# Moving the low-part weight tiles of a two-part float32 matmul kernel from 64 to 76 bytes off the other operands

## The chip, the core and the metric

The kernel runs on one NeuronCore of a Trainium2 chip. The metric is the device time of one execution in microseconds, as the median of several runs: 2093.12 us before the change (three runs, 2093.07 to 2093.68). The profiled execution, from which all durations below are taken, is one more run of the same program.

## What is computed

The reference is a two-layer decoder trunk on 256 tokens of width 2048, all in float32. Cut to its matrix products:

```python
D_MODEL = 2048; SEQ = 256; G_W = 1536; D_FF = 5632; MEM_W = 512; Q_RANK = KV_RANK = 512

def conv_ffn(h, w_up, cw, cb, w_down):          # in both layers
    a = h @ w_up                                 # 2048 -> 11264
    ...
    return (jax.nn.silu(gate) * val) @ w_down    # 5632 -> 2048

# layer 0
z = h @ w_in_a[l]                                # 2048 -> 3584: gate, value, memory queries
main = spatial_gating(z[..., :G_W], z[..., G_W:2 * G_W], g_v[l], w_sp[l], b_sp[l])
# layer 1
z = h @ w_in_b[j]                                # 2048 -> 1024
main = mla_attention(...)                        # low-rank attention with w_uq, w_uk, w_uv
# both layers
mo = memory_attention(q_m, mem, g_mem[l], w_mem_kv[l])
x = x + jnp.concatenate([main, mo], axis=-1) @ w_out[l]
x = x + conv_ffn(rmsnorm(x, g_ffn[l]), w_ffn_up[l], conv_w[l], conv_b[l], w_ffn_down[l])
```

Most of the arithmetic is the two feed-forward blocks (w_ffn_up and w_ffn_down), then w_in_a and w_out.

## The kernel before

**Two parts for each operand.** TensorE multiplies in the type fp32r, which keeps fewer bits than float32. So each operand is split into a high part (the value as fp32r holds it) and a low part (the rest), and a product is the sum of three matmuls: high by high, high by low, low by high. An activation operand is one tile of 128 partitions by 512: the high part of the 256 tokens in the first 256 columns, the low part in the last 256. These tiles are named xhl (the residual stream), h (the hidden layer of the feed-forward block), mainhl, memhl, qhl and chl. A weight chunk of 128 by 1024 arrives in a tile raw by a DMA of 512 KB from SP's queue (`chunk`, L107); ScalarE (ACT) copies it to its high part, tile whi (L117, or L122 with a gain), and VectorE (DVE) subtracts to get the low part, tile wlo (L118, or L123 with a gain). Four buffers of raw, whi and wlo turn over.

**Two ways to run a product.** In `gemm_fm` the weights are the operand that TensorE loads (128 columns), and the activations stream past it. `mm_fm` issues two kinds of matmul: L158 loads a block of whi and streams all 512 columns of the activation tile (high and low together), L162 loads a block of wlo and streams the 256 high columns alone. It issues all L162 of a group of chunks in a row, and all L158 in a row, in alternating order from group to group; away from the ends of a product two groups meet, so that 32 matmuls of one kind follow 32 of the other. In `gemm_tm` it is the other way round: the activations are loaded (128 tokens), and the weights stream, 512 columns wide: L213 (high by whi), L214 (high by wlo), L215 (low by whi). In the last product of the program a few of these are 256 columns wide. A wlo tile is loaded by `gemm_fm`, by the queries' product and by the stacked key weights (L872), and streamed by `gemm_tm`.

**Where the tiles lie.** In this text the place of an operand is its byte address within a partition, modulo 256. The tiles whi, raw, wlo and all six activation tiles begin at place 96. The columns taken from them begin at multiples of 512 bytes, so every operand of L158, L213, L214 and L215 is at place 96. The wlo tile is 1088 columns of 4 bytes long (4352 bytes, 17 times 256), although 1024 are used. `low_tile` returns the first 1024 columns where the tile will stream (`moves=True`), and 1024 columns from the 16th on where it will be loaded. So the wlo weights of L162 and L872 are at place 96 + 64 = 160, and those that stream at 96.

**What sets the order.** A scheduler orders each engine's instructions; only the first product and the last one have an order written out by hand. Semaphores tie a matmul to the DVE and ACT instructions that write its weights, and these to the matmuls that last used the buffer.

Of the kernel before, what the change touches and what calls it, by code (L numbers as in the profile page):

```python
# [69 lines left out]
class Kernel:  # L70
# [21 lines left out]

    def low_tile(self, moves=False):
        w = self.wp.tile([P, 1088], F32R, tag="wlo", name=self.uid("wlo"), bufs=4)
        return w[:, :1024] if moves else w[:, 16 : 16 + 1024]


    def chunk(self, src, nk, ncol, gains=None, heads=None, raw=None, moves=False):
# [1025 lines left out]
```

## Time and profile before

| | before |
|---|---|
| median of three runs | 2093.12 us |
| the profiled execution | 2094.34 us |
| its span, first to last instruction | 2092.6 us |
| TensorE matmul busy (PE) | 2082.2 us |
| weight loads busy (PEld) | 1821.7 us |
| VectorE busy (DVE) | 1458.7 us |
| ScalarE busy (ACT) | 1139.0 us |
| GpSimd busy (POOL) | 398.9 us |
| bytes moved by DMA | 392.01 MB, mean 187 GB/s |
| granted TensorE clock, mean | 0.999 |

The profiled execution is 1.7 us longer than its span, and 1.2 us longer than the median. In the rows of the profile, PE is a matmul and PEld the weight load that goes with it; "ps<-xhl,wlo" is a matmul that reads tiles xhl and wlo and adds to a PSUM tile ps. Loads overlap the matmul before. A matmul's own duration (281 ns, say) is its time from start to modelled end, and matmuls are pipelined, so that the next one starts long before: what counts for the time is the distance from one start to the next, which this text calls the pace. It is read from the timeline view, which merges equal instructions that follow each other: the start of one row less the start of the row before, divided by that row's count.

### The profile page before, as it was taken

How to read it: one execution, taken by the hardware profiler on the slowest of the kernel's cores; microseconds unless marked ns; L12 is line 12 of the kernel's file. 1: busy time of each engine (PE TensorE's matmuls, PEld its weight loads, DVE VectorE, ACT ScalarE, POOL GpSimd, SP SyncE). 2: the span in 40 equal slices, each digit the busy share in tenths (PEclk: the TensorE clock that was granted, in tenths of full speed). 3: DMA queues.
4: the chain of work that ended last, by engine and by line, in shares of the span. 5: the costliest groups of instructions: out<-in, count | busy, mean ns of one | idle time of the engine just before them, and what ended most of it. 6: DMA issues, size and time to landing. Idle time of an engine off the chain costs nothing.

```text
span 2092.6 us, 31012 instructions
## 1 busy us (share of the span) xinstructions
PE 2082.2 (100%) x11614; PEld 1821.7 (87%) x11614; DVE 1458.7 (70%) x2150; ACT 1139.0 (54%) x1747; POOL 398.9 (19%) x387
## 2 busy tenths in 40 slices
PE   9999999999999999999999999999999999999998
PEld 8888888888888888888888888888888888888886
DVE  6755767777756777567798875777765677746775
ACT  6754654555535655445655664456553565535554
POOL 0100133312101211012244121421210122201220
PEclk9999999999999999999999999999999999999999
DMA  8665555656556565556555534555655556555554
GB/s 272 197 216 159 161 195 188 191 188 195 191 192 191 181 201 188 194 185 190 190 192 182 176 106 159 185 190 181 192 194 194 186 188 194 196 196 189 184 191 152
DMA packets 208092, 392.01 MB, mean 187 GB/s; under 512 B 14334, under 2 KB 23876, under 8 KB 207812
## 3 DMA queue, kind: packets, MB, share of 16 engines
q1 hardware_dynamic: 207364, 388.98, 57.3%
q8 instruction: 91, 1.49, 0.3%
q10 hardware_dynamic: 576, 1.05, 0.2%
q14 instruction: 61, 0.50, 0.1%
HBM read 387.88 MB, written 2.10 MB: 186 GB/s over the span
## 4 chain that ended last, share of the span: by engine, by line
PE 99%; DMA 0%; ACT 0%; DVE 0%; issue 0%; ACTq 0%
PE ps L158 51%; PE ps L162 26%; PE ps L215 6%; PE ps L213 6%; PE ps L214 6%; PE ps L949 0%; PE ps L947 0%; PE ps L575 0%; PE ps L610 0%; DMA raw<-in_w_mem_kv 0%; PE ps L432 0%; PE ps L979 0%; PE ps L760 0%; PE ps L872 0%; PE ps L970 0%; PE ps L1051 0%
## 5 line engine op out<-in xcount | busy, mean ns | idle before, releaser
L118 DVE TENSOR_TENSOR wlo<-raw,whi 128x1024 fp32r<-128x1024 f32 x660 | 842.5, 1286 | 468.1 <-ACT whi L117 346.0
L117 ACT ACTIVATE whi<-raw 128x1024 fp32r<-128x1024 f32 x660 | 695.6, 1058 | 692.3 <-PE ps L158 511.3
L158 PE MATMUL ps<-xhl,whi 128*128 128x512 f32 x3264 | 765.0, 390 | 0.0
L158 PEld LDWEIGHTS ps<-xhl,whi 128*128 128x128 f32 x3264 | 605.1, 188 | 121.2
L662 POOL TENSOR_TENSOR a<-js,rbc 128x256 f32<-128x256 f32 x176 | 232.1, 1331 | 1094.1 <-DVE js L264 998.5
L162 PEld LDWEIGHTS ps<-xhl,wlo 128*128 128x128 f32 x3264 | 400.8, 189 | 8.4
L162 PE MATMUL ps<-xhl,wlo 128*128 128x256 f32 x3264 | 404.8, 281 | 0.0
L158 PE MATMUL ps<-h,whi 128*128 128x512 f32 x704 | 164.7, 390 | 0.0
L665 ACT ACTIVATE c<-a,cT 128x256 f32<-128x256 f32 x176 | 105.2, 598 | 98.6 <-POOL a L662 97.0
L158 PEld LDWEIGHTS ps<-h,whi 128*128 128x128 f32 x704 | 130.5, 188 | 26.0
L214 PE MATMUL ps<-wlo,h 128*128 128x512 f32 x354 | 137.1, 388 | 0.0
L213 PE MATMUL ps<-whi,h 128*128 128x512 f32 x354 | 137.0, 388 | 0.0
L215 PE MATMUL ps<-whi,h 128*128 128x512 f32 x354 | 136.6, 388 | 0.0
L158 PE MATMUL ps<-mainhl,whi 128*128 128x512 f32 x512 | 120.1, 390 | 0.0
L158 PEld LDWEIGHTS ps<-mainhl,whi 128*128 128x128 f32 x512 | 94.8, 188 | 18.9
L667 DVE SCALAR_TENSOR_TENSOR c<-a,cT,c 128x254 f32<-128x254 f32 x176 | 101.0, 586 | 0.0
L666 DVE SCALAR_TENSOR_TENSOR c<-a,cT,c 128x255 f32<-128x255 f32 x176 | 91.7, 540 | 12.9 <-ACT c L665 12.7
L123 DVE SCALAR_TENSOR_TENSOR wlo<-raw,gT,whi 128x512 fp32r<-128x512 f32 x112 | 87.1, 819 | 19.3 <-ACT whi L122 17.5
L122 ACT ACTIVATE whi<-raw,gT 128x512 fp32r<-128x512 f32 x112 | 74.7, 723 | 31.6 <-PE ps L158 14.2
L264 DVE TENSOR_TENSOR js<-ps,cr 128x256 f32<-128x256 f32 x209 | 82.2, 415 | 12.4 <-POOL a L662 12.4
L262 ACT ACTIVATE cr<-ps 128x256 f32<-128x256 f32 x243 | 79.7, 374 | 15.7 <-PE ps L158 12.1
L162 PEld LDWEIGHTS ps<-h,wlo 128*128 128x128 f32 x704 | 86.5, 189 | 1.9
(259 smaller groups left out, 1859.6 us busy)
## 6 DMA issues: line engine op xcount, KB each, us to landing
raw<-in_w_ffn_up SPq DMA_DIRECT2D x352, 512.0 KB, 3.5
raw<-in_w_ffn_down SPq DMA_DIRECT2D x176, 512.0 KB, 4.3
raw<-in_w_out SPq DMA_DIRECT2D x64, 512.0 KB, 3.5
raw<-in_w_in_a SPq DMA_DIRECT2D x56, 512.0 KB, 4.0
raw<-in_w_mem_kv SPq DMA_DIRECT2D x31, 512.0 KB, 3.8
raw<-in_w_in_b SPq DMA_DIRECT2D x16, 512.0 KB, 3.5
raw<-in_w_kv_a SPq DMA_DIRECT2D x9, 512.0 KB, 4.2
raw<-in_w_uq SPq DMA_DIRECT2D x12, 384.0 KB, 3.3
```

The costliest lines, as they stand in the source:

```text
L117: nc.scalar.activation(hi[:, :n], raw[:, :n], AF.Copy)
L118: nc.vector.tensor_tensor(lo[:, :n], raw[:, :n], hi[:, :n].bitcast(F32), ALU.subtract)
L123: nc.vector.scalar_tensor_tensor(lo[:, s], raw[:, s], gains[k], hi[:, s].bitcast(F32), ALU.mult, ALU.subtract)
L158: mm(acc[:, :], wh, x, start=first, stop=last)
L162: mm(acc[:, S:], wl, x[:, :S], start=False, stop=False)
L213: mm(acc, xh, wh, start=first, stop=False)
L214: mm(acc, xh, wl, start=False, stop=False)
L215: mm(acc, xl, wh, start=False, stop=last)
L662: nc.gpsimd.tensor_tensor(a, self.join(acc), rb, ALU.mult)
L665: nc.scalar.activation(c, a, AF.Identity, scale=w(2), bias=w(3))
L666: nc.vector.scalar_tensor_tensor(c[:, 1:], a[:, : S - 1], w(1), c[:, 1:], ALU.mult, ALU.add)
L667: nc.vector.scalar_tensor_tensor(c[:, 2:], a[:, : S - 2], w(0), c[:, 2:], ALU.mult, ALU.add)
```

## The change

One number changes: the low part of weights that are loaded begins at column 19 of its tile instead of column 16, so 76 bytes from the tile's start instead of 64, at place 172 instead of 160.

```diff
     def low_tile(self, moves=False):
         w = self.wp.tile([P, 1088], F32R, tag="wlo", name=self.uid("wlo"), bufs=4)
-        return w[:, :1024] if moves else w[:, 16 : 16 + 1024]
+        return w[:, :1024] if moves else w[:, 19 : 19 + 1024]
```

The tile keeps its size, and all tiles keep their addresses. No instruction is added, removed or moved: on all five engines the instructions stand in the same order before and after. What differs is the address of the loaded operand of 4728 matmuls L162 and 8 of the 16 matmuls L872, and the address to which VectorE writes these low parts (L118, L123, and those of the queries and the stacked weights). Streaming low parts (L214) stay at place 96.

## The prediction

> **What bounds the kernel now.** I read the page's busy times first, then the clock, the chain that ended last, and what TensorE waited for.
>
> ```profile
> PE 2082.2 (100%) x11614; PEld 1821.7 (87%) x11614; DVE 1458.7 (70%) x2150; ACT 1139.0 (54%) x1747; POOL 398.9 (19%) x387
> ...
> PEclk9999999999999999999999999999999999999999
> ...
> PE ps L158 51%; PE ps L162 26%; PE ps L215 6%; PE ps L213 6%; PE ps L214 6%; PE ps L949 0%; PE ps L947 0%; PE ps L575 0%; PE ps L610 0%; DMA raw<-in_w_mem_kv 0%; PE ps L432 0%; PE ps L979 0%; PE ps L760 0%; PE ps L872 0%; PE ps L970 0%; PE ps L1051 0%
> ```
>
> ```profile
> PE ps L513 <- DVE ones L312: 1.1, 1, 1.1
> PE ps L356 <- DMA graw<-in_g_mem: 0.3, 1, 0.3
> PE ps L979 <- ACT pT L972: 0.3, 1, 0.3
> PE ps L158 <- DVE memhl L482: 0.2, 1, 0.2
> ```
>
> TensorE is busy over the whole span at a granted clock that never falls, and the waits of its matmuls (second view: total, times, longest) come to 2 us in all. So the time is the sum of TensorE's paces, and nothing else. 26% of the chain is L162, the only large group whose operand the change moves; a nanosecond on its pace counts in full. The groups of L162:
>
> ```profile
> L162 PE MATMUL ps<-xhl,wlo 128*128 128x256 f32 x3264 | 404.8, 281 | 0.0
> ...
> L162 PE MATMUL ps<-h,wlo 128*128 128x256 f32 x704 | 87.0, 281 | 0.0
> L162 PE MATMUL ps<-mainhl,wlo 128*128 128x256 f32 x512 | 63.4, 281 | 0.0
> ...
> L162 PE MATMUL ps<-memhl,wlo 128*128 128x256 f32 x128 | 17.6, 283 | 0.1
> ...
> L162 PE MATMUL ps<-qhl,wlo 128*128 128x256 f32 x72 | 9.7, 280 | 0.0
> ...
> L162 PE MATMUL ps<-chl,wlo 128*128 128x256 f32 x48 | 7.0, 282 | 0.0
> ```
>
> That is 3264 + 704 + 512 + 128 + 72 + 48 = 4728 matmuls. The eight of L872 are too few to matter.
>
> **The pace of L162, in three conditions.** Timeline rows (start, length, engine, line) from the middle of the program, with the low weights 64 bytes off what streams:
>
> ```profile
> 1402.77 3.93 PE L162 MATMUL ps<-xhl,wlo 128*128 128x256 f32 x32
> 1406.54 7.44 PE L158 MATMUL ps<-xhl,whi 128*128 128x512 f32 x32
> 1413.82 3.93 PE L162 MATMUL ps<-xhl,wlo 128*128 128x256 f32 x32
> ```
>
> (1406.54 - 1402.77) / 32 = 117.8 ns for L162, and 7.28 / 32 = 227.5 ns for the 512 wide L158. By this pace the 4728 take 557 us, which agrees with 26% of the span. Second, the end of the last product, where loaded and streaming operands are at one place (0 bytes off) and the matmuls are as wide as L162's:
>
> ```profile
> 2080.76 0.39 PE L214 MATMUL ps<-wlo,h 128*128 128x512 f32 x1
> ...
> 2082.57 0.28 PE L213 MATMUL ps<-whi,h 128*128 128x256 f32 x1
> ...
> 2083.29 0.28 PE L213 MATMUL ps<-whi,h 128*128 128x256 f32 x1
> ```
>
> Six intervals in 0.72 us: 120.0 ns at 0 bytes off. (The eight 512 wide ones before took 1.81 / 8 = 226.3 ns.) Third, a short run of L162 in the attention part, again 64 bytes off:
>
> ```profile
> 1195.40 1.08 PE L162 MATMUL ps<-chl,wlo 128*128 128x256 f32 x8
> 1196.31 0.63 PE L158 MATMUL ps<-chl,whi 128*128 128x512 f32 x2
> ```
>
> 0.91 / 8 = 113.8 ns. So the same instruction on operands at the same places runs at two paces, and equal places are slower than either. The durations (shortest, median, longest) of the same three stretches, in the same order, from the views of the lines in those windows:
>
> ```profile
> L162 PEld LDWEIGHTS ps<-xhl,wlo x32: 187/188/192, 1402.5 to 1406.3; 128*128 128x128 f32 x32
> L162 PE MATMUL ps<-xhl,wlo x32: 280/281/282, 1402.8 to 1406.4; 128*128 128x256 f32 x32
> ```
>
> ```profile
> L214 PEld LDWEIGHTS ps<-wlo,h x4: 188/192/192, 2082.6 to 2083.6; 128*128 128x128 f32 x4
> L214 PE MATMUL ps<-wlo,h x4: 283/283/283, 2082.7 to 2083.8; 128*128 128x256 f32 x4
> ```
>
> ```profile
> L162 PEld LDWEIGHTS ps<-chl,wlo x8: 187/188/188, 1195.2 to 1196.1; 128*128 128x128 f32 x8
> L162 PE MATMUL ps<-chl,wlo x8: 276/276/281, 1195.4 to 1196.2; 128*128 128x256 f32 x8
> ```
>
> The pace goes with two marks: a load that sometimes takes 192 ns instead of 188, and a matmul that takes 276, 281 or 283. At 0 bytes off nearly all loads are long, at 64 bytes some, in the short stretch none.
>
> Last, how fast a load can be repeated when little streams: L760 streams only 128 columns.
>
> ```profile
> 196.83 2.28 PE L760 MATMUL ps<-wT,vn 128*128 128x128 f32 x19
> ...
> L760 PE MATMUL ps<-wT,vn x48: 270/275/275, 189.8 to 208.3; 128*128 128x128 f32 x48
> ```
>
> (2280 - 275) / 18 = 111.4 ns. At 117.8 ns L162 runs 6.4 ns above that.
>
> **How the place can act: a supposition.** A load reads 512 bytes of a partition in about 111 ns, and the matmul that streams meanwhile reads 1024 bytes in about 118, twice as fast. If reads at equal places hinder each other, the stream gains 512 bytes on the load, two rounds of 256, and passes it two or three times: at 0 bytes off the third meeting falls into nearly every load, at 64 bytes it falls at the edge, in some loads and not in others. Twelve bytes more are 12 / 512 x 111.4 = 2.6 ns later. The rows above fit this, but none shows a meeting.
>
> [...]
>
> **The change part by part.** *The loads of L162.* If every third load is long and costs the pace of the 0-byte stretch, the other two run at (3 x 117.8 - 120.0) / 2 = 116.7 ns. The third is an estimate; the group's mean bears on it:
>
> ```profile
> L162 PEld LDWEIGHTS ps<-xhl,wlo 128*128 128x128 f32 x3264 | 400.8, 189 | 8.4
> ```
>
> 189 between 188 and 192 is a quarter of long loads, by rounding an eighth to three eighths. I take it that 2.6 ns moves the edge far enough that no load is long: 1.1 ns x 4728 = 5.2 us saved. Bounds: all of L162 at the pace of the short stretch, (117.8 - 113.8) x 4728 = 18.9 us saved; all at the pace of 0 bytes off, 2.2 x 4728 = 10.4 us lost. The load's own floor, 6.4 x 4728 = 30.3 us, is the furthest a gain can reach; no L162 run at 64 bytes comes near it. I choose the small gain because the fast pace has shown only in short runs, and the nearest row is the 32-long one.
>
> *The start of each L158 run.* Its 227.5 ns against 226.3 at steady pace is 1.2 x 32 = 38 ns for a run of 32, and there are at most 4728 / 32 = 148 such runs: 5.7 us in all that hang on how the low run before has left the loads. It could go or double; I take zero, and keep 5.7 us either way.
>
> *The writes of the low parts.* VectorE writes to the new place. The views of L118 in a window where the tile streams (written to place 96) and one where it is loaded (written to place 160):
>
> ```profile
> L118 DVE TENSOR_TENSOR wlo<-raw,whi x27: 1212/1226/1227, 97.9 to 171.9; 128x1024 fp32r<-128x1024 f32 x27
> ...
> L118 DVE TENSOR_TENSOR wlo<-raw,whi x37: 1210/1224/1764, 899.8 to 999.2; 128x1024 fp32r<-128x1024 f32 x37
> ```
>
> 1226 and 1224 ns: 64 bytes don't show. Operands 4 and 8 bytes off are in L666 and L667, against the aligned L275:
>
> ```profile
> L666 DVE SCALAR_TENSOR_TENSOR c<-a,cT,c x176: 468/476/967, 390.8 to 2030.0; 128x255 f32<-128x255 f32 x176
> L667 DVE SCALAR_TENSOR_TENSOR c<-a,cT,c x176: 467/477/980, 391.6 to 2032.3; 128x254 f32<-128x254 f32 x176
> L275 DVE SCALAR_TENSOR_TENSOR xhl<-ps,gT,xhl x16: 468/478/486, 40.5 to 82.0; 128x256 fp32r<-128x256 f32 x16
> ```
>
> 476, 477 and 478. I take zero. What hides a slower write is VectorE's free time, 2092.6 - 1458.7 = 634 us, over 660 writes of L118 and 112 of L123 0.82 us each; only a write longer by that would reach TensorE.
>
> *Everything else* (order, DMA, ACT, L158's operands, L213 to L215) keeps its addresses and costs nothing.
>
> **The sum.** The profiled execution, 2094.34 us, would become 2089.1; it stands 1.2 us above the median of 2093.12, which would become 2093.12 - 5.2 = 2087.9, say 2088. A measurement of this kernel can tell 0.2%, 4.2 us, from no change: 0.9 ns on L162. With the L158 term the forecast's own range is 2082 to 2092.
>
> **The rivals.**
>
> *The fast pace everywhere (chance 0.24).* 12 bytes also shift the load against the stream by less than one of its long steps, and the short stretch shows that a steady pace without long loads exists. For it: eight intervals at 113.8. Against: at 64 bytes the long runs don't fall into it. Time: 2093.1 - 18.9 = 2074.
>
> *Nothing happens (0.26).* The 32-long runs at 117.8 are a rhythm that loads and matmuls set each other, whatever the small offset: 64 bytes bought only 2.2 ns over 0, so 12 may buy a tenth of that. For it: both paces occur at one offset, so offset isn't all. Against: the 0-byte row. Time: 2093.
>
> *Slower: every low load is long (0.20).* Place 172 is no longer a multiple of 16, as every other operand in these matmuls is. [...] Then L162 runs as at 0 bytes off: 2093.1 + 10.4 = 2103.5. It decides from 0.9 ns per matmul. For it: L162 is where load and stream are most nearly equal, so nothing covers a longer load. Against: no row has a load off a multiple of 16. [...]
>
> *VectorE becomes the bound (0.02)*, by the 0.82 us above; nothing speaks for it.
>
> **How the numbers follow.** The forecast has 0.28. Of it four fifths save more than 4.2 us. Faster: 0.24 + 0.22 = 0.46. Same: 0.26 + 0.06 = 0.32. Slower: 0.22. The likeliest single case is the small gain, 2088. The range takes in the fast pace (2074, less 2 for part of the L158 term) and the long loads (2103.5): 2072 to 2104; both floors beyond are left out.
>
> **What would show it.** The forecast: 32-long L162 runs of 3.73 us, loads 187/188/188, matmuls still near 281. The fast pace: matmuls of 276, runs of 3.64 us. Nothing: 3.77 and 281. Slower: loads of 192 as the median, matmuls of 283 or more, runs of 3.84 us. L213 to L215 must keep 226 ns in every case, and TensorE's waits must stay near 2 us; if either moves, the argument is wrong and not only its size.

## The result, and the profile after

| | before | after |
|---|---|---|
| median | 2093.11 us (four runs, 2093.07 to 2093.68) | 2076.17 us (four runs, 2075.91 to 2076.27) |
| profiled execution | 2094.34 us | 2076.27 us |
| its span | 2092.6 us | 2074.6 us |

The ratio is 0.9918, with a 95% interval from 0.9901 to 0.9935: 0.8% faster, 16.9 us. The two profiled executions lie 18.1 us apart, because the one before stood 1.2 us above its median; no trace shows where those 1.2 us were. The page shows the same picture as before, with less TensorE time in it:

```profile
span 2074.6 us, 31012 instructions
...
PE 2064.0 (99%) x11614; PEld 1803.8 (87%) x11614; DVE 1460.5 (70%) x2150; ACT 1138.7 (55%) x1747; POOL 397.3 (19%) x387
...
PEclk9999999999999999999999999999999999999999
...
PE ps L158 52%; PE ps L162 26%; PE ps L214 6%; PE ps L213 6%; PE ps L215 6%; PE ps L949 0%; PE ps L947 0%; PE ps L575 0%; PE ps L432 0%; PE ps L610 0%; PE ps L979 0%; PE ps L760 0%; PE ps L513 0%; PE ps L872 0%; PE ps L970 0%; PE ps L599 0%
```

TensorE's waits, in the same view as before, are still 2 us in all:

```profile
PE ps L513 <- DVE ones L312: 1.1, 1, 1.1
PE ps L158 <- DVE memhl L482: 0.6, 1, 0.6
PE ps L979 <- ACT pT L972: 0.3, 1, 0.3
```

So the 18.0 us that the span lost must be pace. The view by windows, asked for L162's instructions alone over the whole span, gives their busy time (columns: window, its length, PE busy, PEld busy, clock, DMA share, GB/s), before and then after:

```profile
0.00:2093.00 2093.00, 589.51 (x4728) 583.08 (x4728) 1.00 0.58 187
```

```profile
0.00:2075.00 2075.00, 571.81 (x4728) 566.55 (x4728) 1.00 0.61 189
```

17.7 us less over the 4728 matmuls of L162. The same view for L158, before and then after:

```profile
0.00:2093.00 2093.00, 1113.94 (x4728) 874.75 (x4728) 1.00 0.58 187
```

```profile
0.00:2075.00 2075.00, 1114.07 (x4728) 874.29 (x4728) 1.00 0.61 189
```

L158 hasn't moved. Added up from the start times in the two traces, the distances from each L162 to the matmul behind it come to 558.7 us before and 540.6 us after: 18.0 us, all that the span lost. The gain is L162. Its 32-long run in the timeline, about where the prediction read it, and the durations of its loads and matmuls in that run:

```profile
1389.70 3.80 PE L162 MATMUL ps<-xhl,wlo 128*128 128x256 f32 x32
1393.34 7.44 PE L158 MATMUL ps<-xhl,whi 128*128 128x512 f32 x32
1400.62 0.63 PE L162 MATMUL ps<-xhl,wlo 128*128 128x256 f32 x4
```

```profile
L162 PEld LDWEIGHTS ps<-xhl,wlo x32: 187/188/189, 1389.5 to 1393.1; 128*128 128x128 f32 x32
L162 PE MATMUL ps<-xhl,wlo x32: 276/276/281, 1389.7 to 1393.2; 128*128 128x256 f32 x32
```

3.64 / 32 = 113.8 ns, where it was 117.8; the matmul lasts 276 ns, where it was 281; no load takes 192. L158 keeps its 7.28 / 32 = 227.5 ns. The pace that before showed only in short runs, as in the one of the attention part (113.8 ns), now fills the long ones.

Within such a run the pace isn't the same throughout. A row for 18 matmuls from its middle gives the steady pace: the row's length, less one matmul's own duration, over 17, good to 0.6 ns because a row is rounded to 0.01 us. After:

```profile
1391.19 2.20 PE L162 MATMUL ps<-xhl,wlo 128*128 128x256 f32 x18
```

(2.20 - 0.276) / 17 = 113.2 ns. So the run's average of 113.8 holds some slower distances outside its middle. The same row of the kernel before:

```profile
1393.25 2.28 PE L162 MATMUL ps<-xhl,wlo 128*128 128x256 f32 x18
```

(2.28 - 0.281) / 17 = 117.6 ns. This steady pace is what the experiments are compared by. It holds for the whole program: by the start times in the traces, the 18 distances in the middle of each of the 126 runs of 32 have a mean of 117.8 ns before and 113.3 ns after, and after the change each of these runs begins with three distances of 117 to 119 ns before it settles. VectorE's writes of the low parts kept their median of 1225 ns:

```profile
L118 DVE TENSOR_TENSOR wlo<-raw,whi x660: 1205/1225/1771, 97.0 to 2056.6; 128x1024 fp32r<-128x1024 f32 x165
```

### The profile page after: what moved, and what is told of

It reads as the page before. It is cut to its first block, busy times and chain, and to the rows that moved or that the text cites. A ratio compares the mean times of both kernels' runs of the same rounds, so it can differ in the third digit from the quotient of the medians.

```text
span 2074.6 us, 31012 instructions
## 1 busy us (share of the span) xinstructions
PE 2064.0 (99%) x11614; PEld 1803.8 (87%) x11614; DVE 1460.5 (70%) x2150; ACT 1138.7 (55%) x1747; POOL 397.3 (19%) x387
## 4 chain that ended last, share of the span: by engine, by line
PE 99%; ACT 0%; DVE 0%; issue 0%; ACTq 0%
PE ps L158 52%; PE ps L162 26%; PE ps L214 6%; PE ps L213 6%; PE ps L215 6%; PE ps L949 0%; PE ps L947 0%; PE ps L575 0%; PE ps L432 0%; PE ps L610 0%; PE ps L979 0%; PE ps L760 0%; PE ps L513 0%; PE ps L872 0%; PE ps L970 0%; PE ps L599 0%
## 5 line engine op out<-in xcount | busy, mean ns | idle before, releaser
L118 DVE TENSOR_TENSOR wlo<-raw,whi 128x1024 fp32r<-128x1024 f32 x660 | 842.8, 1287 | 453.2 <-ACT whi L117 338.6
L158 PE MATMUL ps<-xhl,whi 128*128 128x512 f32 x3264 | 765.2, 390 | 0.0
L158 PEld LDWEIGHTS ps<-xhl,whi 128*128 128x128 f32 x3264 | 604.9, 188 | 121.2
L162 PEld LDWEIGHTS ps<-xhl,wlo 128*128 128x128 f32 x3264 | 388.9, 188 | 8.4
L162 PE MATMUL ps<-xhl,wlo 128*128 128x256 f32 x3264 | 392.2, 277 | 0.0
L158 PE MATMUL ps<-h,whi 128*128 128x512 f32 x704 | 164.8, 390 | 0.0
L158 PEld LDWEIGHTS ps<-h,whi 128*128 128x128 f32 x704 | 130.4, 188 | 26.0
L214 PE MATMUL ps<-wlo,h 128*128 128x512 f32 x354 | 137.1, 388 | 0.0
L213 PE MATMUL ps<-whi,h 128*128 128x512 f32 x354 | 137.0, 388 | 0.0
L215 PE MATMUL ps<-whi,h 128*128 128x512 f32 x354 | 136.6, 388 | 0.0
L158 PE MATMUL ps<-mainhl,whi 128*128 128x512 f32 x512 | 120.1, 390 | 0.0
L158 PEld LDWEIGHTS ps<-mainhl,whi 128*128 128x128 f32 x512 | 94.7, 188 | 18.9
L123 DVE SCALAR_TENSOR_TENSOR wlo<-raw,gT,whi 128x512 fp32r<-128x512 f32 x112 | 87.4, 822 | 16.9 <-ACT whi L122 15.3
L162 PEld LDWEIGHTS ps<-h,wlo 128*128 128x128 f32 x704 | 83.9, 188 | 1.9
```

What stands on the lines that cost most here:

```text
L118: nc.vector.tensor_tensor(lo[:, :n], raw[:, :n], hi[:, :n].bitcast(F32), ALU.subtract)
L123: nc.vector.scalar_tensor_tensor(lo[:, s], raw[:, s], gains[k], hi[:, s].bitcast(F32), ALU.mult, ALU.subtract)
L158: mm(acc[:, :], wh, x, start=first, stop=last)
L162: mm(acc[:, S:], wl, x[:, :S], start=False, stop=False)
L213: mm(acc, xh, wh, start=first, stop=False)
L214: mm(acc, xh, wl, start=False, stop=False)
```

## The experiments

Every kernel below differs from the changed kernel by the lines shown, if nothing else is said. Each was run once, with a profile; the kernel before, run beside them on the same chips, took 2093.1 to 2093.9 us. With one run each, the steady paces and busy times carry the argument, and the totals only bear them out. The theories: A, the prediction's supposition, that 64 bytes lie at an edge and a little more gets past it; B, that the remainder modulo 16 is what counts; C, that the place itself counts, not the distance between the two operands.

### 80 bytes off

```diff
-        return w[:, :1024] if moves else w[:, 19 : 19 + 1024]
+        return w[:, :1024] if moves else w[:, 20 : 20 + 1024]
```

> Low weights 80 bytes off (place 176, a multiple of 16). Theory A, the meeting at the edge: 80 is further past the edge than 76, so the long L162 runs settle at 113.3 ns as at 76, run near 2076 us. Theory B, the remainder modulo 16: 80 leaves remainder 0 as 64 does, so L162 stays at 117.8 ns, run near 2093 us.

2097.14 us. 18 matmuls from the middle of a long run, in the timeline and in the view of the line:

```profile
1395.16 2.30 PE L162 MATMUL ps<-xhl,wlo 128*128 128x256 f32 x18
```

```profile
L162 PE MATMUL ps<-xhl,wlo x18: 278/280/282, 1395.2 to 1397.2; 128*128 128x256 f32 x18
L162 PEld LDWEIGHTS ps<-xhl,wlo x18: 187/188/188, 1395.2 to 1397.2; 128*128 128x128 f32 x18
```

(2.30 - 0.28) / 17 = 118.8 ns, slower than at 64. One column of 4 bytes beyond the change undoes all of its gain and more. Theory A falls: 80 is further past its edge. And the loads last 187 to 188 ns at this slow pace, so a slow pace needs no long load: the mark that the prediction read as a cause is none here.

### 12 bytes off

```diff
-        return w[:, :1024] if moves else w[:, 19 : 19 + 1024]
+        return w[:, :1024] if moves else w[:, 3 : 3 + 1024]
```

> Low weights 12 bytes off (place 108): the remainder modulo 16 of the change without its 64 bytes. Theory A: 12 is hardly away from 0, the third meeting falls into nearly every load, L162 near 120 ns, run near 2103 us. Theory B: remainder 12 is what counts, L162 settles at 113.3 ns, run near 2076 us.

2092.67 us.

```profile
1391.87 2.26 PE L162 MATMUL ps<-xhl,wlo 128*128 128x256 f32 x18
```

```profile
L162 PE MATMUL ps<-xhl,wlo x18: 274/278/282, 1391.9 to 1393.9; 128*128 128x256 f32 x18
```

(2.26 - 0.278) / 17 = 116.6 ns: neither 120 nor 113.3. Both theories miss. Matmuls of 274 to 282 ns stand in one run here, where at 76 (below) all last 276: the pace is not one distance repeated. By the start times in the trace, 112 or 113 ns take turns with 120 or 121. The total hardly moved although the pace fell by 1 ns: in the view by windows L162 is busy for 585.08 us, 4.4 less than before the change, but L158 for 1116.67, 2.7 more.

### 128 bytes off

```diff
-        return w[:, :1024] if moves else w[:, 19 : 19 + 1024]
+        return w[:, :1024] if moves else w[:, 32 : 32 + 1024]
```

> Low weights 128 bytes off (place 224), half a round of 256. Theory A: as far from the edge as can be, 113.3 ns, near 2076 us. Theory B: remainder 0 modulo 16, 117.8 ns, near 2093 us.

2105.20 us.

```profile
1389.80 2.32 PE L162 MATMUL ps<-xhl,wlo 128*128 128x256 f32 x18
```

```profile
L162 PE MATMUL ps<-xhl,wlo x18: 281/284/285, 1389.8 to 1391.8; 128*128 128x256 f32 x18
```

(2.32 - 0.284) / 17 = 119.8 ns, worse than 64. This is the furthest from equal places that a round of 256 allows, and it does no good. Theory A is gone; theory B's remainder of 0 (117.8 expected) misses by 2 ns as well.

### All tiles 128 bytes further

```diff
-        self.ident = cp.tile([P, P], F32, name="ident")
+        pad, self.ident = cp.tile([P, 32], F32, name="pad"), cp.tile([P, P], F32, name="ident")
```

> The changed kernel with 128 unused bytes ahead of all other tiles: every tile moves by 128, so all operands are at place 224 and the loaded low weights at 44, still 76 off. If the distance between the operands is what counts (theories A and B alike): 113.3 ns and 2076 us. If the place 172 itself counts (rival C): any other pace, 117.8 ns and 2093 us most likely.

2076.45 us.

```profile
1391.36 2.20 PE L162 MATMUL ps<-xhl,wlo 128*128 128x256 f32 x18
```

```profile
L162 PE MATMUL ps<-xhl,wlo x18: 276/276/276, 1391.4 to 1393.3; 128*128 128x256 f32 x18
```

113.2 ns, as in the changed kernel. The place 172 has no virtue of its own; here the low weights lie at 44. Rival C is out for a shift of 128.

### 76 + 256 bytes off

```diff
-        w = self.wp.tile([P, 1088], F32R, tag="wlo", name=self.uid("wlo"), bufs=4)
-        return w[:, :1024] if moves else w[:, 19 : 19 + 1024]
+        w = self.wp.tile([P, 1152], F32R, tag="wlo", name=self.uid("wlo"), bufs=4)
+        return w[:, :1024] if moves else w[:, 83 : 83 + 1024]
```

> Low weights 332 = 76 + 256 bytes into a longer tile, so at the place 172 of the change. After the first runs theory A and theory B are both gone: 12, 64, 76, 80 and 128 bytes off gave steady L162 paces of 116.7, 117.8, 113.3, 118.7 and 120.0 ns. Theory D: the offset picks a rhythm of loads and matmuls at a grain of 4 bytes and repeats every 256 bytes: 113.3 ns, 2076 us. Rival E: the distance itself counts, not its remainder: another pace, 2085 to 2105 us.

2075.95 us.

```profile
1390.83 2.20 PE L162 MATMUL ps<-xhl,wlo 128*128 128x256 f32 x18
```

113.2 ns again. The effect repeats after 256 bytes; rival E is out.

### 76 + 128 bytes off

```diff
-        return w[:, :1024] if moves else w[:, 19 : 19 + 1024]
+        return w[:, :1024] if moves else w[:, 51 : 51 + 1024]
```

> Low weights 204 = 76 + 128 bytes off. If the round were 128 bytes: 113.3 ns and 2076 us, as at 76. If it is 256 bytes (theory D as I have it): another pace, 116 to 120 ns, 2088 to 2105 us.

2118.75 us, the worst of the runs that moved the low weights alone, and above the range that I expected.

```profile
1387.91 2.38 PE L162 MATMUL ps<-xhl,wlo 128*128 128x256 f32 x18
```

```profile
L162 PE MATMUL ps<-xhl,wlo x18: 286/286/287, 1387.9 to 1390.0; 128*128 128x256 f32 x18
```

(2.38 - 0.286) / 17 = 123.2 ns. A round of 128 bytes is out. The low weights lie at place 44 here, as they did with all tiles 128 bytes further: a load from 44 went with 113.2 ns beside a stream from 224, and with 123.2 beside one from 96. So the load's place doesn't set the pace by itself; it counts together with the stream's.

### 76 + 64 bytes off

```diff
-        return w[:, :1024] if moves else w[:, 19 : 19 + 1024]
+        return w[:, :1024] if moves else w[:, 35 : 35 + 1024]
```

> Low weights 140 = 76 + 64 bytes off, again remainder 12 modulo 16. So far remainder 12 gave 116.7 (12), 113.3 (76) and 123.3 ns (204). If the cost repeats every 64 bytes it would have done so there already, so no round of 64: any pace between 113.3 and 123.3 ns, 2076 to 2122 us; a pace under 113.3 would make it a better version.

2106.14 us.

```profile
1390.17 2.32 PE L162 MATMUL ps<-xhl,wlo 128*128 128x256 f32 x18
```

```profile
L162 PE MATMUL ps<-xhl,wlo x18: 282/283/283, 1390.2 to 1392.2; 128*128 128x256 f32 x18
L162 PEld LDWEIGHTS ps<-xhl,wlo x18: 191/191/191, 1390.2 to 1392.2; 128*128 128x128 f32 x18
```

119.8 ns. Four distances with remainder 12 modulo 16 give 116.6, 113.2, 119.8 and 123.2 ns: the remainder alone decides nothing.

### The high weights 76 bytes off as well

```diff
-        hi = self.wp.tile([P, 1024], F32R, tag="whi", name=self.uid("whi"), bufs=4)
+        hi = self.wp.tile([P, 1088], F32R, tag="whi", name=self.uid("whi"), bufs=4)[:, 0 if moves else 19 :][:, :1024]
...
-            w = self.wp.tile([P, 1024], F32R, tag=tag, name=self.uid(tag), bufs=4) if i == 0 else self.low_tile()
+            w = self.wp.tile([P, 1088], F32R, tag=tag, name=self.uid(tag), bufs=4)[:, :1024] if i == 0 else self.low_tile()
```

> The changed kernel, with the high weights that are loaded (L158) 76 bytes off as well, in tiles of 1088 columns. If 76 is a good distance for any load beside a stream: L158 falls from 226.7 towards 222 ns or less, saving 4728 x 4.4 = 21 us, run near 2055 us. If the rhythm belongs to loads that nearly fill the stream's time (111.4 of 113.3 to 120 ns), L158 with its 512 columns doesn't care: 226.7 ns, 2076 us. L162 stays at 113.3 either way.

2104.00 us. L158's run here lies between the starts of the last two rows:

```profile
1387.31 3.82 PE L162 MATMUL ps<-xhl,wlo 128*128 128x256 f32 x32
1390.96 7.62 PE L158 MATMUL ps<-xhl,whi 128*128 128x512 f32 x32
1398.43 0.76 PE L162 MATMUL ps<-xhl,wlo 128*128 128x256 f32 x5
```

L158 takes 7.47 / 32 = 233.4 ns, where it took 227.5: the distance that helps L162 costs L158 about 6 ns in this run. Over the whole span, L158 first, then L162:

```profile
0.00:2103.00 2103.00, 1139.35 (x4728) 878.14 (x4728) 1.00 0.60 186
```

```profile
0.00:2103.00 2103.00, 573.89 (x4728) 568.92 (x4728) 1.00 0.60 186
```

That is 25.3 us more for L158 and 2.1 us more for L162, nearly all of the total's 27.8 (2104.0 - 2076.2). Neither expectation held. L162's own run averages 3.65 / 32 = 114.1 ns, 0.3 more than in the changed kernel.

### The high weights 64 bytes off

```diff
-        hi = self.wp.tile([P, 1024], F32R, tag="whi", name=self.uid("whi"), bufs=4)
+        hi = self.wp.tile([P, 1088], F32R, tag="whi", name=self.uid("whi"), bufs=4)[:, 0 if moves else 16 :][:, :1024]
...
-            w = self.wp.tile([P, 1024], F32R, tag=tag, name=self.uid(tag), bufs=4) if i == 0 else self.low_tile()
+            w = self.wp.tile([P, 1088], F32R, tag=tag, name=self.uid(tag), bufs=4)[:, :1024] if i == 0 else self.low_tile()
```

> The changed kernel with the loaded high weights 64 bytes off (place 160, a multiple of 16). If L158 is slowed only by loads off a multiple of 16: 226.7 ns or a little less (in the kernel before, a 512 wide matmul followed by a load at 64 took 226 ns), L162 unchanged, run 2070 to 2076 us. If any distance other than 0 slows the 512 wide stream, as 76 did to 233 ns: 230 ns or more, run above 2090 us.

2102.21 us.

```profile
1386.13 3.81 PE L162 MATMUL ps<-xhl,wlo 128*128 128x256 f32 x32
1389.78 7.62 PE L158 MATMUL ps<-xhl,whi 128*128 128x512 f32 x32
1397.24 0.98 PE L162 MATMUL ps<-xhl,wlo 128*128 128x256 f32 x7
```

7.46 / 32 = 233.1 ns, on a multiple of 16. So L158 is slowed without a remainder, too, as the second of the two expectations had it; of three distances tried for it beside a stream at place 96, 0 is the best by 6 ns. No version of the high weights beats the changed kernel.

### Activations at place 84, low weights at 160

```diff
-        self.ap = pool("ap")
+        self.ap = pool("ap"); self.act = lambda tag, dt=F32R: self.ap.tile([P, NB * 512 + 64], dt, tag=tag, name=self.uid("act_" + tag))[:, 61 : 61 + NB * 512]
...
-        return w[:, :1024] if moves else w[:, 19 : 19 + 1024]
+        return w[:, :1024] if moves else w[:, 16 : 16 + 1024]
...
-        self.xhl = self.ap.tile([P, NB, 512], F32R, tag="xhl", name=self.uid("xhl"))
+        self.xhl = self.act("xhl").rearrange("p (k c) -> p k c", k=NB)
```

(The other tiles of the tags xhl and big are taken from the same helper.)

> Low weights back at place 160, 64 bytes into their tile and on a multiple of 16, and the activation tiles xhl, h, mainhl and memhl moved to place 84, so the distance is again 76 while the odd remainder lies with the stream. If the distance alone counts (theory D): L162 settles at 113.3 ns. If the load's own start off a multiple of 16 made the gain: 117.8 ns. The distance of L158's operands becomes 12 and that of L213 to L215 minus 12, which no run has had, so the total is open by 10 us either way; L162 is to be read alone.

2166.93 us.

```profile
1392.96 4.00 PE L162 MATMUL ps<-act_big,wlo 128*128 128x256 f32 x32
1396.80 4.00 PE L158 MATMUL ps<-act_big,whi 128*128 128x512 f32 x16
1400.64 3.99 PE L158 MATMUL ps<-act_xhl,whi 128*128 128x512 f32 x16
1404.46 0.76 PE L162 MATMUL ps<-act_xhl,wlo 128*128 128x256 f32 x5
```

L162 takes 3.84 / 32 = 120.0 ns at a distance of 76, neither of the two paces expected: the distance alone doesn't make the fast pace. L158 takes 7.66 / 32 = 239.4 ns, but its distance became 12 and its stream left the multiples of 16 together, and this run can't tell the two apart.

### L162's stream alone at place 84

To the kernel before, with the low weights at place 160:

```diff
-                mm(acc[:, S:], wl, x[:, :S], start=False, stop=False)
+                mm(acc[:, S:], wl, x[:, 61 : 61 + S], start=False, stop=False)
```

> The kernel before (low weights at place 160), with L162 alone streaming columns 61 to 316 of the activation tile instead of 0 to 255, so from place 84: its distance is 76, its stream starts off a multiple of 16, L158 is untouched. It multiplies the wrong columns, and is run for its time alone. If the distance alone sets L162's rhythm: 113.3 ns, run near 2076 us. If it matters which of the two starts off a multiple of 16, and the pace seen with the activation tiles moved was L162's own and not inherited from a disturbed L158: 120 ns, near 2103 us.

2119.03 us.

```profile
1388.81 2.38 PE L162 MATMUL ps<-xhl,wlo 128*128 128x256 f32 x18
```

```profile
L162 PE MATMUL ps<-xhl,wlo x18: 287/288/289, 1388.8 to 1390.9; 128*128 128x256 f32 x18
L162 PEld LDWEIGHTS ps<-xhl,wlo x18: 192/193/193, 1388.8 to 1390.9; 128*128 128x128 f32 x18
```

(2.38 - 0.288) / 17 = 123.1 ns, again neither of the paces expected. Here the load stayed where it was in the kernel before, L158 too, and only the place from which L162 streams moved: 117.6 became 123.1 ns. So the pace hangs on both operands' places. And the same two places, 84 and 160, gave 120.0 ns in the run before this one and 123.1 here: a pair of places has more than one pace, as 64 bytes had two in the kernel before (113.8 in the short run, 117.8 in the long).

### Both operands of L162 16 bytes further

```diff
-        return w[:, :1024] if moves else w[:, 19 : 19 + 1024]
+        return w[:, :1024] if moves else w[:, 23 : 23 + 1024]
...
-                mm(acc[:, S:], wl, x[:, :S], start=False, stop=False)
+                mm(acc[:, S:], wl, x[:, 4 : 4 + S], start=False, stop=False)
```

> The changed kernel with both operands of L162, and no others, 16 bytes further: the stream from column 4 of the activation tile (place 112), the low weights 92 bytes into their tile (place 188). The distance is 76 and the remainders modulo 16 are 0 and 12 as in the change; L158 keeps its places. It multiplies partly wrong columns, and is run for its time alone. If distance and remainder modulo 16 of L162's two operands set its rhythm: it settles at 113.3 ns, run near 2076 us. If coarser places or the relation to L158's operands count too: 116 to 123 ns, 2088 to 2120 us.

2107.17 us.

```profile
1391.70 2.32 PE L162 MATMUL ps<-xhl,wlo 128*128 128x256 f32 x18
```

```profile
L162 PE MATMUL ps<-xhl,wlo x18: 278/280/285, 1391.7 to 1393.7; 128*128 128x256 f32 x18
```

(2.32 - 0.28) / 17 = 120.0 ns. Distance and remainders are those of the change, and yet its pace is not there, as the second expectation had it. A common shift of 128 bytes of all tiles left the pace at 113.2 ns, a common shift of 16 of these two costs 6.8 ns.

### Together

| L162 streams from | loads from | distance | steady ns | run, us |
|---|---|---|---|---|
| 96 | 108 | 12 | 116.6 | 2092.67 |
| 96 | 160 | 64 (before) | 117.6 | 2093.11 |
| 96 | 172 | 76 (after) | 113.2 | 2076.17 |
| 96 | 172 | 332 | 113.2 | 2075.95 |
| 224 | 44 | 76, all tiles moved | 113.2 | 2076.45 |
| 96 | 176 | 80 | 118.8 | 2097.14 |
| 96 | 224 | 128 | 119.8 | 2105.20 |
| 96 | 236 | 140 | 119.8 | 2106.14 |
| 96 | 44 | 204 | 123.2 | 2118.75 |
| 112 | 188 | 76, L162 alone moved | 120.0 | 2107.17 |
| 84 | 160 | 76, L162's stream alone moved | 123.1 | 2119.03 |
| 84 | 160 | 76, activations moved, L158 slower too | 120.0 | 2166.93 |
| 96 | 172 | 76, high weights at 76, L158 slower | 113.2 | 2104.00 |
| 96 | 172 | 76, high weights at 64, L158 slower | 113.2 | 2102.21 |

Where L158 keeps its places, the time of the program follows the steady pace of L162: from 113.2 to 123.2 ns is 10.0 x 4728 = 47 us by the paces, and 2118.75 - 2076.17 = 43 us measured. It follows roughly only, because not every run of L162 is long enough to settle (66 of the 192 have 2 to 24 matmuls, the others 32) and because L158 moves by up to 4 us as well (1117.98 us busy at 140 bytes off, 1114.07 after the change).

What stays open is what inside the chip makes 76 from 96 the good one. Two explanations are left for the two common shifts, by 128 and by 16 bytes: the places themselves count, modulo 32, 64 or 128 bytes, or the relation of L162's stream to L158's counts, which the shift of all tiles kept and the shift of 16 did not. Moving L158's loads (high weights at 64 or 76) left L162 at its steady 113.2 ns, so at least its relation to those is not it. All tiles shifted by 16, 32 or 64 weren't tried, nor a stream that stays in one place.

## Why the prediction was right, and where it was not

*The number.* The time fell, as forecast, and the stated range held, because it was wide enough for the rivals as well. The forecast itself, 2088 with a range of its own of 2082 to 2092, was missed, and the reason given for a gain falls below. That this shift gained was luck: of the six distances tried in place of 64 with nothing else moved, only 76 gained clearly, 12 left the total about where it was, and 80, 128, 140 and 204 lost.

*What bounds.* Right. The waits stayed at 2 us, and the span's 18.0 us are in L162's own rows.

*What is untouched.* Right: L158 at 227.5 ns including the slower start of its runs (the 5.7 us that could have gone or doubled did neither, though at 140 bytes off L158 took 4 us more), VectorE's writes at 1225 ns. L213 to L215 kept their pace, too: ten 512 wide ones from the end of the timeline after take 2.27 / 10 = 227 ns.

```profile
2062.24 0.39 PE L215 MATMUL ps<-whi,h 128*128 128x512 f32 x1
...
2064.51 0.28 PE L213 MATMUL ps<-whi,h 128*128 128x256 f32 x1
```

*The size.* This is the term that was mis-sized. The prediction took the pace from 117.8 to 116.7 ns, 5.2 us; it went to 113.8, 4.0 x 4728 = 18.9 us by the long runs and 17.7 by all of L162's rows. The short runs gained less; the 48 matmuls on chl, by the view of the line after (shortest, median, longest), kept their median of 281 ns:

```profile
L162 PE MATMUL ps<-chl,wlo x48: 276/281/364, 1172.2 to 1239.9; 128*128 128x256 f32 x48
```

The pace of 113.8 is that of the first rival, at 2074, to which the prediction gave 0.24; the median came out at 2076.17. Both of that rival's signs are there, matmuls of 276 ns and runs of 3.64 us. Its bound, the short run of the attention part, was the right row to read. The reason for leaving it, that the nearest row was the long run at 117.8, was wrong: that row carried the old places, and at new places the row said nothing. Nor was the fast pace as short-lived as it seemed. The kernel before holds it for 14 matmuls on mainhl:

```profile
1281.92 1.75 PE L162 MATMUL ps<-mainhl,wlo 128*128 128x256 f32 x14
L162 PE MATMUL ps<-mainhl,wlo x14: 276/276/276, 1281.9 to 1283.4; 128*128 128x256 f32 x14
```

(1.75 - 0.276) / 13 = 113.4 ns, at the places 96 and 160 where the runs of 32 went at 117.8.

*The supposition.* Wrong in its step "at 64 bytes it falls at the edge": with meetings that slide past an edge 80 and 128 bytes would be as good as 76 (113.2 ns), and at 118.8 and 119.8 ns they are worse than 64 (117.6). The one in three long loads, on which 116.7 rested, was counted about right (by the trace before, 30% of L162's loads last 191 or 192 ns) but didn't set the pace: at 80 bytes no load of the run above is long and the pace is 118.8. Nor did long loads cost the pace of the 0-byte stretch in the kernel before: in its runs of 32 every distance is 117 to 119 ns, none 120 and none 116.7. Only the outer frame held: the places of the two operands count together, and 256 bytes more left the pace at 76 at 113.2 ns. The frame is shown by the runs in which one operand moved at a time (the low weights, from 113.2 to 123.2 ns; or, with the load at 160, L162's stream, from 117.6 to 123.1), by the load from 44 with its two paces, 113.2 and 123.2 ns, and by the runs at 76 + 256 and 76 + 128, 113.2 and 123.2 ns. That the two reads hinder each other was a supposition, and no run shows the reads.

*The slower rival.* That a load off a multiple of 16 takes longer and L162 with it: no. The fastest pace of all, 113.2 ns, has such a load, with 187 to 189 ns. Off multiples of 16 there are both the best and the worst of the runs that moved the low weights alone: 113.2 ns at 76 bytes off, 123.2 at 204. Of the two floors that the range leaves out, no run shows a term for the one on the slow side; what the runs showed beyond this rival's 120.0 ns is 123.2 ns at 204 bytes off (2118.75 us) and 123.1 where L162's stream alone moved (2119.03 us).

## What to carry to other kernels

In this kernel the address of the loaded tile modulo 256 against that of the streaming tile moved the pace of matmuls with 256 columns by 9%, from 113 to 123 ns, with no other line of the program changed; moving the loads of the 512 wide ones cost 6 of 227 ns. No simple rule came out of the places tried. So scan them in steps of one element (4 bytes made 113.2 into 118.8 ns here), for each shape of matmul by itself (the best distance for 256 columns, 113.2 ns, was a bad one for 512, 233.4 for 227.5), and again when tiles move by anything but a multiple known to be harmless (128 bytes of everything here: 113.2 ns, 2076.45 us). Read the pace from the start-to-start distance in the middle of a long run, not from the instructions' durations, and don't carry the pace of a short run over to a long one: at the same places, 96 and 160, the two were 113.8 and 117.8 ns here.

## What the runs showed that I had not expected

**One pair of places has several paces.** In the kernel before, 13 of the 192 runs of L162 reach 113 to 114 ns, none of them longer than 17 matmuls, while all 126 runs of 32 go at 117.8. The kernel after, too, has another pace at its places: a run of 12 on memhl that follows two matmuls of L458.

```profile
61.29 1.24 PE L162 MATMUL ps<-memhl,wlo 128*128 128x256 f32 x9
L162 PE MATMUL ps<-memhl,wlo x9: 282/283/284, 61.3 to 62.2; 128*128 128x256 f32 x9
```

(1.24 - 0.283) / 8 = 119.6 ns. And at 76 + 128 bytes off, the slowest place of the low weights, a run of 16 on memhl that follows transposes (L432) settles at the fast pace:

```profile
64.11 1.30 PE L162 MATMUL ps<-memhl,wlo 128*128 128x256 f32 x10
L162 PE MATMUL ps<-memhl,wlo x10: 276/276/278, 64.1 to 65.1; 128*128 128x256 f32 x10
```

(1.30 - 0.278) / 9 = 113.6 ns, good to 1.1, where the runs of 32 of that kernel go at 123.2. So the places don't fix the pace alone. What the change did is that the runs of 32, which begin right behind L158, now settle at the pace that a few short runs had already. The first two matmuls of both runs shown here start about 200 ns apart; that the beginning of a run picks its pace fits this, but was not tried by itself. It may also be why the places 84 and 160 gave 120.0 ns in one kernel and 123.1 in the other.

**The steady paces are averages.** By the start times in the traces, the means over the middles of the runs of 32 are 113.3 ns at 76 bytes off, 116.7 at 12, 117.8 at 64, 118.7 at 80, 120.0 at 128 and 140, and 123.3 at 204. Four of these six are multiples of 3.33 ns (34 to 37 of them); 117.8 and 118.7 are not. The single distances are mostly no such multiples: at 12 they take turns between 112 or 113 and 120 or 121 ns, at 204 between 120 or 121 and 125 or 126, at 64 they lie between 117 and 119, and only at 76 (113 or 114 ns) and 140 (120 ns) are they all alike. Why the means fall so is open.
